# A two-layer encoder with four mixers: ten projection steps beside the scan, windowed attention and latent keys beside the latent attention

## The chip, the cores and the metric

The kernel runs on one core of a Trainium2 chip. The metric is the device time of one execution in microseconds (us). TensorE appears as PE (matmuls) and PEld (weight loads), VectorE as DVE, ScalarE as ACT, GpSimd as POOL, SyncE, which issues the DMAs here, as SP.

## The reference

1024 tokens of 1024 features pass through two layers in fp32. A layer projects its input once and hands the parts to four mixers of 256 features each; what follows (group norm, output projection, MLP, per-layer embedding) is not touched here.

```python
for i in range(DEPTH):                                  # 2
    u = h @ w_in[i]
    (cq, ckv, kr, hy_u, sq, sk, sv, ssd_z, ssd_xbc, ssd_dt) = jnp.split(u, IN_OFFSETS, axis=-1)
    y_a = mla_mixer(cq, ckv, kr, ...)                   # latent attention, 4 heads, all keys
    y_b = hyena_mixer(hy_u, ...)                        # two long convolutions by transforms
    y_c = swa_mixer(sq, sk, sv, ...)                    # windowed attention, 2 groups of keys, 4 heads
    y_d = ssd_mixer(ssd_xbc, ssd_dt, ...) * silu(ssd_z) # chunked scan, both directions
    y = group_rms_norm(concatenate([y_a, y_b, y_c, y_d]), mix_norm_g[i], 4)
    h = layer_norm(ALPHA * h + y @ w_out[i], ...)
    ...
```

Here mla normalises the latents (cq, ckv), projects them to queries, keys and values and attends over all 1024 keys; swa attends over 128 tokens to either side, with a sink; the scan works in 8 chunks of 128 tokens.

## The kernel before, in words

The kernel is written with generators: each mixer is a flow that yields between steps, `interleave` (L43) emits several flows in step with one another by the numbers of steps given with them, and `stagger` (L55) runs items of one flow one stage apart. A tile scheduler then reorders the instructions of each engine by its own model, within what the data and the buffers allow, so the emission is a wish and not the order.

`mixers` (L580) writes a layer's mixers as three stages. The **input stage** interleaves `hyena` with `proj`: 21 tiles of 128 features, each of 48 matmuls of 512 columns (`in_proj` L564; high and low parts of weights and activations make three products for each of 8 blocks and 2 halves) into a tile `pp` of 1024 columns; a row of 48 such products is named pp<-x,wh or pp<-x,wl. A tile is copied by ScalarE to `cv` and stored to DRAM (`plain` L607: L612; `latent` L615: L620, with token sums of squares `csq` on PE). T_Z (2 tiles) are the gates of the scan, T_CQ (2) and T_CKV (1) the latents of mla, T_SQ, T_SK, T_SV the input of swa, T_X, T_B, T_C that of the scan. Hyena ends with the product of `x2` and its result and two stores of y (L707).

The **scan stage** interleaves `ssd` (L822), `swa` (L1084) and `mla_keys` (L947), the latter held back by 34 empty steps. `ssd` loads xs, bs and cs again (L826) into tiles `xbc`; its first part, the states, makes token-major x and B (`xt`), `xd` = x by a decay, and their product; its second part, 16 outputs, makes Lm (exponentials), `wt` = the sum of two of them (one row wt<-Lm each), the products ps<-wt,xt, and an addition into xbc. Its tiles xbc, prev and xt come from the tag X of the pool `xp`, where the layer's input x also lies, and `PT` and `kT` of mla later. swa has two kv groups; each loads its rows, makes KH, KL and Q and then 8 blocks: scores in a `pp` tile (pp<-KH,Q), softmax (`ws`), transposes into another `pp` tile, `wpt`, and products with `sV`. `mla_keys` makes `kT` and `V` from the latent `ck`.

The **mla stage** interleaves `mla` (L984) with `out_ahead`, which prepares the output projection of Hyena's group. mla has 32 units (4 pairs of query tiles, 4 heads, 2 tiles): scores of 6 matmuls of 512 columns into a `pp` tile, maximum, `P` = exponentials (1024 columns), transposes (L1054), split into `PT`, and the products with V (L942).

PSUM: `one()` gives a `ps` tile of 512 columns out of 4 buffers, `two()` a `pp` tile of 1024 columns out of 2; projections, swa's scores and transposes and mla's scores all take `pp`. Weight rows are loaded to `wraw` (2 buffers) and split by POOL into `wh` and `wl` (`whl`, 4 buffers).

Of the kernel before, what the change touches and what calls it, by code (L numbers as in the profile page):

```python
# [10 lines left out]
F32 = mybir.dt.float32  # L11
# [6 lines left out]
RIGHT = "right"  # L18
# [10 lines left out]
# columns of the packed per-layer parameters  # L29
# [4 lines left out]
# feature tiles of the input projection  # L34
# [8 lines left out]
def interleave(*flows):  # L43
    """Emits flows, each (generator, number of its steps), in step with one another."""
    live = [[g, 0, n] for g, n in flows]
    while live:
        f = min(live, key=lambda f: f[1] / f[2])
        try:
            next(f[0])
            f[1] += 1  # L50
        except StopIteration:
            live.remove(f)


def stagger(items):  # L55
    """Emits the stages of items so that each item is one stage behind the one before it."""
# [18 lines left out]
class Trunk:  # L75
# [70 lines left out]
    def to_x_after(self, x, H, t0, t1, ins, pair=False):  # L146
        """Transposes token tiles t0 to t1, once the products up to ins have freed the tiles that the
        result goes to."""
# [11 lines left out]
    def layer_norm(self, h, gb, eps=None, first=None):  # L160
        """The statistics; returns two functions that normalise h in place, one after the other."""
# [16 lines left out]
        def affine(c=512):  # L178
            """The first c columns, scaled already, on GpSimd, the others on VectorE."""
# [74 lines left out]
    def embed(self):  # L254
        """Normalises the input; the second half of the tokens only when the function that is returned runs."""
# [43 lines left out]
    def sin_of(self, fp, out, pre):  # L299
        """out = sin(pre) with the argument brought to [-pi, pi]."""  # L300
# [99 lines left out]
    def bruun(self, pool, zm, zp, C):  # L400
        """Residues of a polynomial of 1024 coefficients (8 blocks of 128 rows, C columns each)
        modulo the eight factors of x^2048 - 1 of degree 256; zm and zp are its residues modulo
        x^1024 - 1 and x^1024 + 1."""
# [36 lines left out]
    def conv_fft(self, l, n, pool, z, feature_major, out):  # L440
        """Circular convolution of z (token-major, 8 x 256) with filter n, and the skip term that the
        filter holds; the result is token-major [128, 8 * 256] or feature-major [128, 2, 8 * 128]."""
# [112 lines left out]
    def in_half(self, x, w, ps, hf):  # L555
        c0 = hf * 512
        if not isinstance(w, tuple):
            # the products of the high and the low parts of the weights, in separate rows
# [5 lines left out]
    def in_proj(self, l, x, tile_i):  # L564
        """One tile of 128 features, [128, 1024] in PSUM, in two steps."""
# [7 lines left out]
    def conv3(self, out, ps, cw):  # L573
        """Centred 3-tap convolution along the free dim with bias: cw columns w0, w1, w2, b."""
# [4 lines left out]
    def mixers(self, l, x, mu, late, st0):  # L579
# [6 lines left out]
        res, sw = {}, ExitStack()  # L586
        ss = self.sm.tile([128, 4, 8], F32, name="ss")

        def scalars(su, ps):
            """Rotary key and dt, token-major."""  # L590
# [24 lines left out]
        def latent(pr, ti, k, rs, last, n):  # L615
            """A latent of attention with its gain, to DRAM; the sums of its squares go to rs."""
# [16 lines left out]
        def proj(pr, su, head, v, x1):  # L633
# [42 lines left out]
            for i in range(2):  # L676
                yield from plain(pr, T_SQ + i, qd[:, i])
                yield
            for i in range(2):
# [4 lines left out]
            yield from latent(pr, T_CKV, 2, res["rk"], True, 128)  # L684
            yield
            for i in range(2):
                yield from plain(pr, T_Z + i, zd[:, i], AF.Silu)
                yield
# [23 lines left out]
        with ExitStack() as ssu:  # L712
            with ExitStack() as st:
# [14 lines left out]
                interleave((hyena(st, v, x1), 54), (proj(pr, su, head, v, x1), 42))  # L728
            m1 = self.pool(st0, f"m1_{l}")
            w2 = self.pool(sw, f"w2_{l}", 2, side=RIGHT)  # L730
            att = {}
            with ExitStack() as st:
                mc = self.pool(st, f"mc{l}", 2)
                interleave((self.ssd(l, st, res["scal"], xbc, zd, yd[3]), 44), (self.swa(l, w2, yd[2], qd, kd, vd), 32),
# [1069 lines left out]
```

## Time and profile before

| what | value |
|---|---|
| median of 3 runs | 3237.84 us (3234.51 to 3241.9) |
| span of the profiled execution | 3236.6 us |
| difference of the median to that span | 1.2 us |
| PE busy, share of the span | 2976.9 us, 92% |
| VectorE, ScalarE, POOL | 76%, 40%, 56% |

The profile is of one execution; its span is the time that the sum is made against. A window is a stretch of the span in us from its start; the busy time of an engine in it says how much of it the engine worked, PEclk the share of full clock that was granted. A mark is one row of the timeline with its start.

### The profile page before, as it was taken

The numbers are of one execution on the slowest core, as the hardware profiler recorded it, in microseconds if no ns is written. First come the engines' busy times: TensorE is split into PE (matmuls) and PEld (weight loads), VectorE is DVE, ScalarE is ACT, GpSimd is POOL, SyncE is SP. The second block draws the span as 40 slices with busy tenths as digits, with TensorE's granted clock in tenths as the row PEclk, the third lists the DMA queues.
The fourth block names the chain that finished last, engine by engine and source line by source line (L and its number), as shares of the span: only waits on it lengthen the run. The fifth ranks groups of instructions, "written<-read, shape, count | busy, mean of one in ns | idle before, by whom it ended". The sixth has DMA issues, their size and how long they took to land.

```text
span 3236.6 us, 40462 instructions
## 1 busy us (share of the span) xinstructions
PE 2976.9 (92%) x14316; PEld 2429.1 (75%) x14316; DVE 2451.0 (76%) x3711; ACT 1292.0 (40%) x2278; POOL 1821.3 (56%) x1371
## 2 busy tenths in 40 slices
PE   6999989998999999999989998899989999989996
PEld 4887866877777777777868877778777777767685
DVE  7678776878765557999777786778786555689986
ACT  4332365743333334333343323667333333343341
POOL 5455533527656556886435454345177555578855
PEclk9999998999999999999999998999999999999998
DMA  5566523022222225313335755130222222343232
GB/s 178 156 200 204 192 75 130 16 83 85 85 79 78 78 79 198 123 47 115 126 100 172 225 192 165 53 121 25 97 85 79 79 78 78 114 163 107 74 135 92
DMA packets 140468, 368.98 MB, mean 114 GB/s; under 512 B 15139, under 2 KB 42023, under 8 KB 140009
## 3 DMA queue, kind: packets, MB, share of 16 engines
q1 hardware_dynamic: 126008, 315.72, 28.8%
q0 software_dynamic: 14256, 50.67, 5.2%
q8 instruction: 114, 1.87, 0.2%
q14 instruction: 90, 0.73, 0.1%
HBM read 278.77 MB, written 87.56 MB: 113 GB/s over the span
## 4 chain that ended last, share of the span: by engine, by line
PE 39%; DVE 21%; POOL 16%; issue 10%; DMA 10%; ACT 4%; SPq 0%; POOLq 0%; DVEq 0%; ACTq 0%
PE ps L99 18%; PE pp L99 13%; POOL w L87 5%; DMA wraw<-in_ffn_w_gate_dram 4%; POOL wraw L87 4%; DVE part L87 3%; POOL u L87 2%; DVE fr L87 2%; POOL H L87 2%; PE ps L942 2%; DVE H L90 2%; DVE s L87 1%; POOL part L87 1%; DVE H L87 1%; DMA wraw<-in_ffn_w_up_dram 1%
## 5 line engine op out<-in xcount | busy, mean ns | idle before, releaser
L99 PE MATMUL ps<-x,w 128*128 128x512 f32 x2112 | 508.2, 394 | 11.3 <-ACT v L84 6.1
L99 PEld LDWEIGHTS ps<-x,w 128*128 128x128 f32 x2112 | 400.1, 190 | 99.1 <-ACT v L84 7.0
L99 PE MATMUL pp<-x,wh 128*128 128x512 f32 x1344 | 427.9, 397 | 1.8 <-ACT wh L84 1.8
L99 PE MATMUL ps<-xq,w 128*128 128x512 f32 x1584 | 391.1, 397 | 29.7 <-DVE u L87 24.3
L1582 PE MATMUL ps<-part 128*128 128x512 f32 x1440 | 351.2, 399 | 33.8 <-DVE H L87 10.8
L99 PEld LDWEIGHTS ps<-xq,w 128*128 128x128 f32 x1584 | 292.9, 188 | 117.2 <-DVE u L87 50.7
L1582 PEld LDWEIGHTS ps<-part 128*128 128x128 f32 x1440 | 270.9, 191 | 110.5 <-DVE H L87 20.3
L99 PEld LDWEIGHTS pp<-x,wh 128*128 128x128 f32 x1344 | 254.9, 192 | 54.3 <-ACT wh L84 2.0
L87 POOL TENSOR_TENSOR w<-wraw,w 128x512 fp32r<-128x512 f32 x164 | 217.5, 1345 | 116.0 <-ACT w L84 116.0
L99 PE MATMUL pp<-x,wl 128*128 128x512 f32 x672 | 266.5, 397 | 3.8 <-POOL wl L87 3.8
L84 ACT ACTIVATE w<-wraw 128x512 fp32r<-128x512 f32 x264 | 151.8, 622 | 268.0 <-DMA wraw<-in_ffn_w_up_dram 218.6
L87 POOL TENSOR_TENSOR wl<-wraw,wh 128x1024 fp32r<-128x1024 f32 (+2 forms) x61 | 152.8, 2507 | 182.7 <-ACT wh L84 124.2
L87 POOL TENSOR_TENSOR part<-fr,part 128x512 fp32r<-128x512 f32 x120 | 192.4, 1628 | 47.2 <-ACT part L84 42.2
L87 DVE TENSOR_TENSOR s<-wraw 128x512 f32<-128x512 f32 x44 | 55.4, 1259 | 202.2 <-DMA wraw<-in_ffn_w_gate_dram 199.8
L99 PE MATMUL ps<-wo,yn 128*128 128x512 f32 x768 | 189.7, 405 | 5.4 <-DVE H L90 3.0
L1039 POOL TENSOR_TENSOR P<-P,smr 128x1024 f32<-128x1024 f32 x64 | 121.1, 1893 | 112.2 <-DVE smr L1038 103.3
L99 PEld LDWEIGHTS ps<-wo,yn 128*128 128x128 f32 x768 | 147.1, 195 | 39.4 <-DVE H L90 4.8
L90 DVE SCALAR_TENSOR_TENSOR g<-g,pp 128x1023 f32<-128x1023 f32 x88 | 126.6, 1439 | 57.7 <-ACT g L84 57.7
L87 POOL TENSOR_TENSOR u<-u,g 128x512 f32<-128x512 f32 x44 | 78.7, 1788 | 152.5 <-ACT g L84 152.3
L87 DVE TENSOR_TENSOR part<-wr,part 128x512 fp32r<-128x512 f32 x124 | 158.2, 1299 | 4.8 <-ACT part L84 4.8
L99 PE MATMUL ps<-wh,x 128*128 128x512 f32 x512 | 158.8, 391 | 0.0
L99 PEld LDWEIGHTS pp<-x,wl 128*128 128x128 f32 x672 | 128.5, 191 | 30.5 <-POOL wl L87 4.7
(381 smaller groups left out, 7038.7 us busy)
## 6 DMA issues: line engine op xcount, KB each, us to landing
c_fwd<-in_c_fwd_dram POOLq DMA_DIRECT2D x64, 512.0 KB, 5.1
wraw<-in_ffn_w_up_dram SPq DMA_DIRECT2D x50, 512.0 KB, 3.5
wraw<-in_ffn_w_gate_dram SPq DMA_DIRECT2D x44, 512.0 KB, 4.5
f<-u SPq DMA_DIRECT2D x88, 256.0 KB, 2.0
wraw<-in_w_in_dram SPq DMA_DIRECT2D x42, 512.0 KB, 4.1
fr<-f SPq DMA_DIRECT2D x40, 512.0 KB, 4.5
wr<-in_ffn_w_down_dram SPq DMA_DIRECT2D x36, 512.0 KB, 6.4
c_inv<-in_c_inv_dram POOLq DMA_DIRECT2D x32, 512.0 KB, 5.0
```

The costliest lines, as they stand in the source:

```text
L84: self.nc.scalar.activation(out, in_, func, **kw)
L87: (eng or self.nc.vector).tensor_tensor(out, a, b, op=op)
L90: return self.nc.vector.scalar_tensor_tensor(out, a, s, b, op0=op0, op1=op1)
L99: ins = self.nc.tensor.matmul(out, a, b, start=i == 0, stop=i == n - 1)
L942: ins = self.nc.tensor.matmul(out[0:64] if j else out, v[:, 0, :] if j else v.rearrange("p i d -> p (i d)"), terms[i][1 + j], start=k == 0 ...
L1039: nc.gpsimd.tensor_tensor(P, P, sm.to_broadcast([128, T]), op=ALU.mult)
L1582: nc.tensor.matmul(ps, u, v, start=k == 0 and (p != 1 or ch == 0), stop=k == 5 and (p != 1 or ch == last))
```

## The change

The five tiles T_Z, T_CKV and T_CQ (10 steps) leave `proj` for a flow `proj_late` that is emitted beside `ssd`. `ssd` gets a pool of its own (`sb`, seven tiles of 8 KB a partition) in place of the tag X, since the layer's input is still read beside it. swa and the latent keys leave the scan stage: the keys become the first part of the flow `attention`, and swa is a third flow beside it; the 34 empty steps go. The pools of swa, keys and mla are opened when those of the scan are closed. Comments are removed as well, which shifts the lines (L826 is L832, L707 is L710, L846 and L847 are L852 and L853, L942 is L948, L1016 is L1020, L1054 is L1058, L1094 is L1098, L1149 is L1153).

```diff
         def proj(pr, su, head, v, x1):
...
-            for i in range(2):
-                yield from latent(pr, T_CQ + i, i, res["rq"], i, 256)
-                yield
-            rq = res["rq"]
-            nc.vector.tensor_scalar(rq, rq, 96.0 ** -0.5, None, op0=ALU.mult)
-            yield from latent(pr, T_CKV, 2, res["rk"], True, 128)
-            yield
-            for i in range(2):
-                yield from plain(pr, T_Z + i, zd[:, i], AF.Silu)
-                yield
+
+        def proj_late(pr):
+            for i in range(2):
+                yield from plain(pr, T_Z + i, zd[:, i], AF.Silu)
+                yield
+            yield from latent(pr, T_CKV, 2, res["rk"], True, 128)
+            yield
+            for i in range(2):
+                yield from latent(pr, T_CQ + i, i, res["rq"], i, 256)
+                yield
+            rq = res["rq"]
+            nc.vector.tensor_scalar(rq, rq, 96.0 ** -0.5, None, op0=ALU.mult)
...
-                interleave((hyena(st, v, x1), 54), (proj(pr, su, head, v, x1), 42))
-            m1 = self.pool(st0, f"m1_{l}")
-            w2 = self.pool(sw, f"w2_{l}", 2, side=RIGHT)
+                interleave((hyena(st, v, x1), 54), (proj(pr, su, head, v, x1), 32))
+            with ExitStack() as st:
+                interleave((self.ssd(l, st, res["scal"], xbc, zd, yd[3]), 44), (proj_late(self.pool(st, f"pl{l}", 2)), 10))
+        rows, ahead = {}, {}
+
+        def attention(mc, m1, m2):
             att = {}
-            with ExitStack() as st:
-                mc = self.pool(st, f"mc{l}", 2)
-                interleave((self.ssd(l, st, res["scal"], xbc, zd, yd[3]), 44), (self.swa(l, w2, yd[2], qd, kd, vd), 32),
-                           (self.mla_keys(l, mc, m1, att, cd, res), 50))
-            sw.close()
-        rows, ahead = {}, {}
+            yield from self.mla_keys(l, mc, m1, att, cd, res)
+            yield from self.mla(l, m2, att, yd[0])
...
         with ExitStack() as sa:
+            w2 = self.pool(sa, f"w2_{l}", 2, side=RIGHT)
+            m1 = self.pool(sa, f"m1_{l}")
+            mc = self.pool(sa, f"mc{l}", 2)
             m2 = self.pool(sa, f"m2_{l}", 2)
-            interleave((self.mla(l, m2, att, yd[0]), 40), (out_ahead(), 36))
+            interleave((attention(mc, m1, m2), 48), (self.swa(l, w2, yd[2], qd, kd, vd), 44), (out_ahead(), 36))
...
     def ssd(self, l, ss, scal, xbc, zd, yd):
...
+        sb = self.pool(ss, f"sb{l}")
         for j in range(3):
-            pair = self.xp.tile([128, 2, T], F32, name="xbc", tag="X")
+            pair = sb.tile([128, 2, T], F32, name=f"xbc{j}")
...
-            prev.append(self.xp.tile([128, 8, 2, 128], F32, name="prev", tag="X"))
-            xt.append(self.xp.tile([128, 8, 2, 128], F32, name="xt", tag="X"))
+            prev.append(sb.tile([128, 8, 2, 128], F32, name=f"prev{g}"))
+            xt.append(sb.tile([128, 8, 2, 128], F32, name=f"xt{g}"))
...
     def mla_keys(self, l, mc, m1, att, cd, res):
...
-        for _ in range(34):
-            yield
```

How the instructions then stand on an engine is the scheduler's doing, and both layers read alike; the rows below are of layer 0. SP's queue at the end of the input stage, before (y is Hyena's result, sk, sq and sv the input of swa, xs, bs and cs that of the scan, kt a row of Hyena's filter spectra, ab a table of swa):

```order
L457 DMA kt<-khat_7_90 128x2x256
L620 DMA cq_275<-cv 128x1024
L1105 DMA wraw<-sk_273 64x1024 x2
L707 DMA y_267<-x_2609 256x1x512 x2
L1098 DMA ab<-in_c_alibi_dram 128x768
L1108 DMA wraw<-sq_272 128x1024
L612 DMA z_271<-cv 128x1024
L826 DMA xbc<-xs_276 128x1024 x2
L826 DMA xbc<-bs_277 128x1024 x2
L826 DMA xbc<-cs_278 128x1024 x2
```

and now:

```order
L457 DMA kt<-khat_7_90 128x2x256
L710 DMA y_267<-x_2402 256x1x512 x2
L832 DMA xbc_3203<-xs_276 128x1024 x2
L832 DMA xbc_3206<-bs_277 128x1024 x2
L832 DMA xbc_3209<-cs_278 128x1024 x2
L612 DMA z_271<-cv 128x1024 x2
L620 DMA cq_275<-cv 128x1024
L931 DMA wraw<-xs_276 128x1024
L620 DMA cq_275<-cv 128x1024
L929 DMA xbc_3209<-z_271 128x1024
```

swa's rows are gone from here, and the six loads of the scan stand directly behind the stores of y, ahead of the stores of two Z tiles and of the latents. Since the tile of xs lies where Hyena's x2 was, its load waits for the y stores.

PE at the same place. Before, the last 111 of Hyena's 640 products in the layer had 30 and 18 projection matmuls (and the sums csq) between them, and 96 behind the last. Now nothing stands between them. The two Z tiles are projected before them, in the input stage; the 144 matmuls of the three latent tiles stand behind the last product, 96 of them in five pieces (22, 4, 23, 27, 20) with the first transposes and state products of the scan between the pieces, the other 48 further on in the scan. PE's rows around the scan's first transposes (L852, L853), now:

```order
L99 MATMUL pp<-x,wl 128x512
L99 MATMUL pp<-x,wh 128x512
L852 MATMUL ps<-ident,xbc_3203 128x128 x2
L99 MATMUL pp<-x,wh 128x512
L99 MATMUL pp<-x,wl 128x512
L99 MATMUL pp<-x,wh 128x512 x2
L853 MATMUL ps<-ident,xbc_3206 128x128 x2
```

They stand behind 22 of the 96 here.

PE at the end of the scan, before (ps<-wt,xt: product of an output of the scan; L906: its transpose; L976: transposes of the keys; sV: products of swa; cn: queries):

```order
L1149 MATMUL pp<-ident,ws 128x128 x4
L99 MATMUL ps<-wt,xt 128x256
L976 MATMUL ps<-ident,ks 96x128 x4
L99 MATMUL ps<-wh,ck 128x512
L99 MATMUL ps<-wl,ck 128x512
L99 MATMUL ps<-wh,ck 128x512
L99 MATMUL ps<-wpt,sV 64x256 x3
L976 MATMUL ps<-ident,ks 96x128 x4
L99 MATMUL ps<-wpt,sV 64x256 x3
L976 MATMUL ps<-ident,ks 96x128 x4
L99 MATMUL ps<-wpt,sV 64x256 x5
L99 MATMUL ps<-wh,cn_5068 128x384
```

and now (csq: the sums of the latents; L1098: transposes of swa's values; ck: keys):

```order
L912 MATMUL ps<-ident,yo 128x128 x2
L99 MATMUL ps<-wt,xt_3218 128x256 x2
L912 MATMUL ps<-ident,yo 128x128
L99 MATMUL ps<-ones,csq 128x1 x4
L99 MATMUL ps<-wt,xt_3218 128x256
L99 MATMUL ps<-ones,csq 128x1 x4
L1098 MATMUL ps<-ident,wraw 128x128 x8
L99 MATMUL ps<-wh,ck 128x512
L99 MATMUL ps<-wl,ck 128x512
L99 MATMUL ps<-wh,ck 128x512 x2
L99 MATMUL ps<-wl,ck 128x512
L99 MATMUL ps<-wh,ck 128x512
L99 MATMUL pp<-KH,Q_4320 128x256
L99 MATMUL pp<-KL,Q_4320 128x256
```

No row of swa or of the keys stands before the scan's last product; their tiles (V, sV, Q, KH and others) lie on tiles of the scan. Behind it come swa's whole first kv group, 106 of swa's 204 matmuls as the rows count them, and the keys, and only then mla's first scores. The second kv group stands between mla's units:

```order
L99 MATMUL pp<-kT,qT_4805 128x512 x2
L99 MATMUL pp<-kT,qT_4806 128x512
L99 MATMUL pp<-kT,qT_4805 128x512 x2
L99 MATMUL pp<-kT,qT_4806 128x512
L99 MATMUL pp<-KH,Q_4846 128x384
L99 MATMUL pp<-KL,Q_4846 128x384
L99 MATMUL pp<-KH,Q_4847 128x384
L99 MATMUL pp<-KL,Q_4847 128x384
L1058 MATMUL ps<-ident,P 128x128 x16
L99 MATMUL pp<-kT,qT_4821 128x512 x2
L99 MATMUL pp<-kT,qT_4822 128x512
L99 MATMUL pp<-kT,qT_4821 128x512 x2
L99 MATMUL pp<-kT,qT_4822 128x512
```

In these rows the scores of a block of swa and the transposes of two units (L1058) stand between the scores of one unit of mla and those of the next. Before, mla's matmuls had nothing beside them but the queries and the sums of `out_ahead`. The eight loads of the residual for the output projection, which stood at mla's start in SP's queue, now stand late in mla, since their tiles lie where swa's are.

## Rows read from the trace of the kernel before

**Rows 1.** The page's busy time of each engine, us, share of the span and instructions.
```profile
PE 2976.9 (92%) x14316; PEld 2429.1 (75%) x14316; DVE 2451.0 (76%) x3711; ACT 1292.0 (40%) x2278; POOL 1821.3 (56%) x1371
```

**Rows 2.** Windows, layer 0: stretch, length, busy PE, PEld, DVE, ACT, POOL, PEclk, DMA, GB/s.
```profile
390.00:409.00 19.00, 17.96 (x87) 14.44 (x85) 8.28 (x20) 6.85 (x9) 6.07 (x7) 1.00 0.92 319
409.00:526.00 117.00, 101.21 (x565) 79.66 (x566) 88.97 (x300) 73.48 (x233) 39.47 (x42) 0.93 0.17 54
526.00:548.00 22.00, 17.38 (x64) 10.26 (x63) 12.44 (x26) 9.80 (x20) 9.06 (x6) 0.77 0.73 255
548.00:662.00 114.00, 109.52 (x720) 97.58 (x720) 94.47 (x187) 82.80 (x153) 61.25 (x37) 0.97 0.12 41
662.00:674.00 12.00, 10.12 (x65) 8.70 (x66) 9.06 (x14) 6.22 (x12) 3.60 (x3) 1.00 0.28 93
```

**Rows 3.** Timeline, marks of layer 0: start us, us, engine, line, operation, out<-in, shapes.
```profile
390.44 1.24 SPq L707 DMA_DIRECT2D y<-x  x2
...
409.10 0.43 DVE L87 TENSOR_TENSOR xd<-ps,s_w 128x256 f32<-128x256 f32 x1
...
525.47 0.29 DVE L87 TENSOR_TENSOR xbc<-ps,yt 64x128 f32<-64x128 f32 x1
...
547.59 1.20 ACT L84 ACTIVATE P<-pp,mx,rq 128x1024 f32<-128x1024 f32 x1 [5.03 <-issue]
...
673.97 0.45 SPq L1065 DMA_DIRECT2D y<-yt  x1
```

**Rows 4.** Windows of layer 1, the scan, same columns as rows 2.
```profile
2006.00:2123.00 117.00, 101.34 (x565) 79.54 (x564) 88.51 (x301) 73.52 (x233) 39.48 (x42) 0.91 0.18 55
```

**Rows 5.** Chain of waits, end of the input stage, layer 0: start us, us, what.
```profile
351.23 6.83 PE pp L99 x30
...
389.37 13.96 PE pp L99 x61
```

**Rows 6.** DMA issues from 385 to 412 us: KB each, median us to landing.
```profile
y<-x SPq DMA_DIRECT2D x2, 512.0 KB, 4.0
...
xbc<-bs SPq DMA_DIRECT2D x2, 512.0 KB, 8.9
```

**Rows 7.** Timeline of VectorE, four of the scan's 16 Lm sums.
```profile
443.04 0.41 DVE L87 TENSOR_TENSOR wt<-Lm 128x256 f32<-128x256 f32 x1
...
494.30 0.43 DVE L87 TENSOR_TENSOR wt<-Lm 128x256 f32<-128x256 f32 x1
...
504.10 0.43 DVE L87 TENSOR_TENSOR wt<-Lm 128x256 f32<-128x256 f32 x1 [0.67 <-PE ps L99]
...
511.84 0.43 DVE L87 TENSOR_TENSOR wt<-Lm 128x256 f32<-128x256 f32 x1
```

**Rows 8.** Waits of PE in the scan, 409 to 526 us: total, times, longest.
```profile
PE ps L99 <- DVE xd L87: 8.8, 4, 3.8
```

**Rows 9.** Timeline, the first and last rows of swa's first kv group.
```profile
405.07 0.36 PE L99 MATMUL pp<-KH,Q 128*128 128x256 f32 x1
...
446.29 0.81 ACT L84 ACTIVATE wpt<-pp 128x768 f32<-128x768 f32 x1 [1.37 <-PE ps L99]
```

**Rows 10.** Timeline of PE, swa's score, transpose and value matmuls.
```profile
422.12 0.34 PE L99 MATMUL pp<-KL,Q 128*128 128x384 f32 x1
422.29 0.33 PE L99 MATMUL pp<-KH,Q 128*128 128x384 f32 x1
...
434.46 0.82 PE L1149 MATMUL pp<-ident,ws 128*128 128x128 f32 x6
...
436.28 1.51 PE L99 MATMUL ps<-wpt,sV 128*64 128x256 f32 x6
```

**Rows 11.** Waits of PE beside mla, 548 to 662 us.
```profile
PE pp L99 <- ACT P L84: 4.9, 4, 2.8
```

**Rows 12.** Timeline, score matmuls of two of mla's units and the exponentials of the first.
```profile
548.94 5.49 PE L99 MATMUL pp<-kT,qT 96*128 96x512 f32 x12 [2.81 <-ACT P L84]
...
555.60 1.20 ACT L84 ACTIVATE P<-pp,mx,rq 128x1024 f32<-128x1024 f32 x1
```

More of the change, by code (lines that the diff above doesn't have):

```diff
@@ L585, in mixers @@
         xbc = [dr(n, [128, 2, T]) for n in ("xs", "bs", "cs")]
-        res, sw = {}, ExitStack()
+        res = {}
         ss = self.sm.tile([128, 4, 8], F32, name="ss")
```

## The prediction

> **What bounds the kernel now.** I read the page's busy shares first. TensorE (PE) is busy for 92% of the span, no other engine for more than 76% [rows 1], so a stage is as long as its matmuls plus the idle time of PE in it. The table of windows by stage comes next, layer 0 with its marks from the timeline [rows 2, 3]: PE is busy 17.96 of 19 us at the end of the input stage, 101.21 of 117 us in the scan, 17.38 of 22 us between the scan and the latent attention (mla), and 109.52 of 114 us in mla. Layer 1 reads the same (scan: 101.34 of 117) [rows 4]; I work out one layer and double it. The idle time that a better mixture could use is thus some 16 us in the scan and some 10 elsewhere. The clock that the throttle granted, 0.93 in the scan, 0.77 after it, 0.97 beside mla [rows 2], is lowest where PE has most idle time; a number below full speed is a mean of the 2.4 and the 1.2 GHz level.
>
> The marks of layer 0 are: y of Hyena goes to its store at 390.44, the first xd of the scan at 409.10, the scan's last addition 525.47, mla's first P (exponentials of a score tile) 547.59, the last store of mla 673.97 [rows 3]. I forecast each distance between two marks anew.
>
> **Term 1, up to the first xd.** The chain of waits at the end of the input stage runs through projections: 30 matmuls of 6.83 us, and later 96 behind the last inverse product of Hyena, the last 61 of them from 389.37 on [rows 5]. By the order, the last 111 Hyena matmuls had 30 and 18 projection matmuls between them; now none. The 96 behind the last inverse product are there still: the scheduler pulls two of the five "moved" tiles back. So 3 tiles (144 matmuls) move at all, and only 48 of them, at 6.83/30 = 0.228 us, 10.9 us in all, leave Hyena's path. The chain shows the 30 on it and not the 18, so I take 6.8 us off: Hyena's y goes out at 383.6. (Bounds: 0, if VectorE, which holds the chain in between, takes all of it, and 10.9.) Behind y SP's queue now holds the six scan loads at once, where a weight row, a table, a latent and one Z store stood between them; and the loads must wait for the y store, since their tile lies over x2. The y store takes 4.0 us from issue, a pair of xbc loads 8.9 beside the other traffic [rows 6]. With a DMA share of 0.92 there already [rows 2] I take 4.0 + 6.5 (8.9 less the two transfers that no longer share the queue) + 1 for transpose and copy: first xd at 395 instead of 409. **-14 us.** With 8.9 whole and only half of the 6.8 gained it would be -8; with all 10.9 gained -17.
>
> **Term 2, the scan.** From 409.10 to 525.47 it took 116.4 us [rows 3], with the swa steps and the latent keys on the same engines. Its own pace is seen where little stands beside it: the Lm sums, one for each of 16 outputs, come 3 intervals apart between 494.30 and 504.10, 3.27 us each; the states before them take 443.04 - 409.10 = 33.9 us [rows 7]. PE waited 8.8 us for xd there [rows 8], a chain through ScalarE and VectorE that swa's softmax lengthens. Without swa I put the states at 31, 15 intervals of 3.27 make 49, the addition and copies after the last output 7 (511.84 to 525.47 is 13.6 with swa and keys in between), and of the 48 moved matmuls' 10.9 us 8 that find no idle PE: 95 us. **-21 us.** Bounds: 85 (states 28, no cost for projections) and 110 (13.6 of tail stay, the interval is 4). The weight splits of the late tiles lie on GpSimd, busy 39.47 of 117 us [rows 2]; that is their cover, with much to spare.
>
> **Term 3, from the scan's end to mla's first P.** It was 22.1 us [rows 3], filled with the end of swa and of the keys. Now neither has begun when the scan ends: their pool lies on tiles of the scan that are still read, and by the order PE has no row of either before the scan's last matmul. Then the whole first kv group of swa, 106 of its 204 rows, stands ahead of mla's first scores. Beside the scan that group took 446.29 + 0.81 - 405.07 = 42 us [rows 9], call it 41. The scan is gone, but all the keys now stand in the same stretch. I take 5 for the transposes and splits of keys and queries, 40 for group and keys together, 4 for the first scores and their maximum: 49 us. **+27 us.** Bounds 40 (PE fed well by two independent flows) and 60 (the clock stays low as in the 0.77 stretch [rows 2]).
>
> **Term 4, mla itself.** It took 126.4 us to the last store [rows 3]. It now shares PE with the second kv group: 32 score matmuls 0.17 us apart, 44 transposes at 0.82/6 = 0.14, 44 value records at 1.51/6 = 0.25 [rows 10], so 5.4 + 6.0 + 11.1 = 22.5 us. Of PE's idle time there (114 - 109.5 = 4.5; the waits for P are 4.9 [rows 2, 11]) they can use 4.5 at most: 18. I add 5 for the score tiles, since swa takes its own from the same two PSUM buffers that mla's use. **+23 us.** Bounds 15 and 46. PE's busy time is the row against which I count room; the row beside it, of weight loads, has 97.58 of 114 us [rows 2]. The Trainium skill would have that one used: "Perfetto Trace Analysis" (Identifying the Most-Contended Engine) calls matmul busy time a poor measure of how near TensorE is to its limit, because matmuls are pipelined, and takes the busy share of weight loads. By it 16 us of mla would be free, term 4 would be 22.5 - 16 + 5 = +12, and the sum 3268 - 22 = 3246 us. No row here shows mla taking more work into those 16 us, so the sum goes by the matmul row. VectorE (94.47 of 114) and ScalarE (82.80) take swa's other half without becoming the bound. The weight and residual loads of the next stage, which stood at mla's start, wait for swa's pool now; beside mla the DMA share is 0.12 to 0.28 [rows 2], so I cost them at nothing; were that cover gone, one load pair's 8.9 us [rows 6] is the price.
>
> **The sum.** -14 - 21 + 27 + 23 = +15 per layer, +30 for two. The profiled span is 3236.6 us, 1.2 below the median of the three runs, 3237.84; 3236.6 + 30 + 1.2 = **3268 us**.
>
> **Rival 1: the two PSUM buffers bind.** mla makes a unit every 114/32 = 3.56 us [rows 2], and a score tile lives from the first of its matmuls (548.94) to the end of its P (555.60 + 1.20), 8 us [rows 12]: two buffers at 3.56 us each give 7.1, so they are full all the time. Then swa's second group does not slip in between; it holds the buffers as long as the first did, 41 us. Term 4 is +41, a layer +33, the time 3238 + 66 = 3304 us. Against it: PE's waits for P are 4.9 us only [rows 11], so the tiles live long because PE is busy. What the Trainium skill says in "Perfetto Trace Analysis" (Optimization Strategy) is on its side: the same gap repeated for a stretch can mean too little SBUF or PSUM for the next tile. The four waits of up to 2.8 us are such gaps, but few. Chance 0.17.
>
> **Rival 2, faster: two full mixtures.** PE was 96% busy beside mla (109.52/114) against 87% in the scan. From 390 to 674 PE's busy time is 17.96 + 101.21 + 17.38 + 109.52 + 10.12 = 256.2 us [rows 2]; with the 10.9 of the moved matmuls 267.1. If every stage were filled as mla was, they need 267.1/0.961 = 278 us, and from 383.6 the layer's mla ends at 661.6 instead of 674: -12.4 per layer, 3238 - 25 = 3213 us. It decides for this if term 3 is near 40 and term 4 below 20 while the scan takes 88. For it: projections have no chain of their own and fit any gap of the scan. Against: 106 rows of swa stand ahead of mla with a softmax chain and nothing but the keys beside it. The Trainium skill speaks for this rival ("Perfetto Trace Analysis", Optimization Strategy): where the most-contended engine changes over time, interleaving the regimes may help; here PE is first in every stage, so the rule bears on its idle time only. Chance 0.22.
>
> **Rival 3: it washes out.** Part of the change isn't carried out (two tiles of five stay where they were). With terms 3 and 4 nearer their lower ends, +18 and +15, a layer is -14 - 21 + 18 + 15 = -2, the time 3234 us. Chance 0.11.
>
> **Numbers.** The forecast has 0.50, the rivals 0.17, 0.22 and 0.11. What a measurement of this kernel can tell from no change is about 0.2%, 6.5 us. Faster by more: rival 2, and a little of rival 3: 0.23. Within: most of rival 3 and the near end of the forecast: 0.13. Slower: 0.64. The range goes from 3210 (just under rival 2) to 3306 (just over rival 1); what is left out is the forecast's tail with every term at its upper bound. The slower case alone would span 3248 to 3306.
>
> **What would show it.** In the changed profile: y of Hyena to its store some 7 us earlier than 390.44 (the input stage's own gain); first xd near 395; the scan about 95 us with short waits for xd; then a stretch of 45 to 50 us in which PE is busy for well under nine tenths and does swa and keys only; mla 150 us long with PE's waits for P grown above 4.9 us. I am wrong if the gap between the scan and the first P is nearer 30 (swa then did overlap), if the scan stays over 110 (then it had been bound by its own chain, not by its neighbours), or if PE beside mla stays as long as 126 us with swa in it.

## The result, and the profile after

The changed kernel takes 3327.78 us in the median of 4 runs (3323.24 to 3334.45), the kernel before 3236.18 us beside it: a ratio of 1.0284, 95% interval 1.0263 to 1.0306. It is slower, as forecast, but by some 92 us where I had 30, and outside the range (3210 to 3306). The page of the profiled execution, span and busy time, against [rows 1]:

```profile
span 3332.6 us, 40443 instructions
...
PE 3003.7 (90%) x14316; PEld 2441.2 (73%) x14316; DVE 2448.9 (73%) x3711; ACT 1292.1 (39%) x2278; POOL 1812.8 (54%) x1371
```

The instruction count of PE is the same, 14316. Its busy time grew by 3003.7 - 2976.9 = 27 us, though nothing was added, and the rest of the span, 3332.6 - 3003.7 = 329 us, is 69 us more than before (3236.6 - 2976.9 = 260). So 69 of the 96 us between the two profiled spans are time in which PE stands still; the other 27 are the same matmuls taking longer, in part at a lower granted clock (last section).

The marks of layer 0 on the timeline, which answer to [rows 3]:

```profile
397.26 1.22 SPq L710 DMA_DIRECT2D y<-x  x2
...
410.85 0.42 DVE L87 TENSOR_TENSOR xd<-ps,s_w 128x256 f32<-128x256 f32 x1 [13.61 <-ACT xt L84]
...
505.42 0.28 DVE L87 TENSOR_TENSOR xbc<-ps,yt 64x128 f32<-64x128 f32 x1 [0.38 <-PE ps L99]
...
568.50 1.20 ACT L84 ACTIVATE P<-pp,mx,rq 128x1024 f32<-128x1024 f32 x1 [4.45 <-DVE mx L1038]
...
726.70 0.45 SPq L1069 DMA_DIRECT2D y<-yt  x1
```

And the windows between them, columns as in [rows 2]:

```profile
397.00:411.00 14.00, 3.45 (x10) 2.47 (x11) 0.39 (x2) 0.57 (x2) 0.00 (x0) 0.63 0.77 254
411.00:506.00 95.00, 87.22 (x479) 73.33 (x477) 47.78 (x160) 39.09 (x122) 15.48 (x20) 0.95 0.22 75
506.00:568.00 62.00, 44.47 (x222) 31.28 (x221) 46.27 (x117) 40.60 (x100) 31.26 (x25) 0.89 0.38 107
568.00:727.00 159.00, 146.56 (x906) 123.65 (x907) 123.97 (x274) 105.47 (x210) 75.53 (x47) 0.96 0.16 53
```

Between Hyena's store and the first xd PE is busy 3.45 of 14 us, where it had 17.96 of 19; the scan is shorter; the hand-over to mla takes 62 us with PE busy 44.47 of them; mla takes 159 us at 146.56. Against the four terms of the prediction, with the same marks in layer 1 (before: last store of layer 0 at 673.97, then 2006.28, 2122.96, 2143.60, 2269.22; after: 726.70, then 2048.66, 2145.12, 2205.34, 2362.14):

| term, us per layer | forecast | layer 0 | layer 1 |
|---|---|---|---|
| 1, up to the first xd | -14 | +1.8 | -10.4 |
| 2, the scan | -21 | -21.8 | -20.2 |
| 3, scan's end to mla's first P | +27 | +41.0 | +39.6 |
| 4, mla | +23 | +31.8 | +31.2 |
| sum | +15 | +52.7 | +40.2 |

Layer 1's first term counts from the end of layer 0's mla, so it holds the rest of layer 0 as well. The two sums and 3 us behind the last mark are the 96 us. Over both layers the terms missed by 19 (term 1), 0 (term 2), 27 (term 3) and 17 us (term 4).

**Why the first term failed** is seen on PE. Its timeline behind Hyena's last product:

```profile
396.07 0.39 PE L99 MATMUL pp<-x,wh 128*128 128x512 f32 x1
406.03 0.66 PE L852 MATMUL ps<-ident,xbc 128*128 128x128 f32 x2 [9.57 <-DMA xbc<-xs]
406.34 0.78 PE L99 MATMUL pp<-x,wh 128*128 128x512 f32 x1
...
409.91 0.69 PE L853 MATMUL ps<-ident,xbc 128*128 128x128 f32 x2 [1.52 <-DMA xbc<-bs]
```

22 projection matmuls run, then stands the scan's transpose of xbc, which waits 9.57 us for its load, and behind it in PE's queue 122 projection matmuls that need none of these loads (emitted ahead of the transposes, they keep PE busy: "Late projections ahead of the scan" below). This is the order that the section on the change shows, and I read it as "the 96 are there still". The waits of PE from 340 to 411 us (total, times, longest) add others:

```profile
PE ps L852 <- DMA xbc<-xs: 9.6, 1, 9.6
PE ps L99 <- DMA c_inv<-in_c_inv_dram: 5.2, 1, 5.2
PE ps L99 <- ACT ph L84: 3.3, 1, 3.3
...
PE ps L99 <- ACT w L84: 1.4, 1, 1.4
```

The last three are Hyena's own: two steps on ScalarE (ph, w), and a load of its inverse transform, c_inv, 5.2 us, which the kernel before did not wait for here. GpSimd, and not SyncE, issues these loads; its timeline just before:

```profile
357.88 2.40 POOL L87 TENSOR_TENSOR wl<-wraw,wh 128x1024 fp32r<-128x1024 f32 x1 [5.29 <-ACT wh L84]
360.23 0.57 POOL L397 DMA_DIRECT2D c_fwd<-in_c_fwd_dram  x1
360.83 1.30 POOL L87 TENSOR_TENSOR rl<-v,rh 128x512 fp32r<-128x512 f32 x1
362.07 1.10 POOL L397 DMA_DIRECT2D c_inv<-in_c_inv_dram  x2
```

The weight split of a late tile (wl) stood 5.29 us for ScalarE's half, and the c_inv loads came behind it, at 362.07; PE, done at 362.5, went on at 367.75. With fewer projections between its products Hyena ran ahead of its loads here; whether this wait moved its end is taken up with the weight splits below.

### The profile page after: what moved, and what is told of

The parts are those of the page before. It is cut to its first block, busy times and chain, and to the rows that moved or that the text cites. A ratio compares the mean times of both kernels' runs of the same rounds, so it can differ in the third digit from the quotient of the medians.

```text
span 3332.6 us, 40443 instructions
## 1 busy us (share of the span) xinstructions
PE 3003.7 (90%) x14316; PEld 2441.2 (73%) x14316; DVE 2448.9 (73%) x3711; ACT 1292.1 (39%) x2278; POOL 1812.8 (54%) x1371
## 5 line engine op out<-in xcount | busy, mean ns | idle before, releaser
L99 PE MATMUL pp<-x,wh 128*128 128x512 f32 x1344 | 442.5, 406 | 12.2 <-ACT cv L84 6.3
L99 PEld LDWEIGHTS pp<-x,wh 128*128 128x128 f32 x1344 | 262.0, 197 | 68.3 <-ACT cv L84 6.9
```

Source lines behind the costliest of these rows:

```text
L99: ins = self.nc.tensor.matmul(out, a, b, start=i == 0, stop=i == n - 1)
```

## The experiments

All times are medians, with the kernel before measured on the same chip beside them (3230.97 to 3234.14 us). Windows are of layer 0, columns as in [rows 2].

**Attention and keys alone.** The kernel before, with windowed attention and the latent keys moved beside mla as in the change, and the projections left where they were. The 34 empty steps go here too.

```diff
-                interleave((self.ssd(...), 44), (self.swa(...), 32), (self.mla_keys(...), 50))
+                interleave((self.ssd(...), 44))
...
-            interleave((self.mla(l, m2, att, yd[0]), 40), (out_ahead(), 36))
+            interleave((attention(mc, m1, m2), 48), (self.swa(l, w2, yd[2], qd, kd, vd), 44), (out_ahead(), 36))
```

> Only windowed attention and the latent keys are moved; the projections stay in the input stage as before, with 96 of their matmuls between Hyena's last product and the scan. Theory A (moving the projections gained nothing, since Hyena's end is set by its own loads and VectorE steps; the whole loss is the hand-over, +41 us, and mla, +32 us per layer, less what the scan saves): input stage and first xd as before at 409, the scan near 87 us (95 less the 8 of late projections), so per layer -29 + 41 + 32 = +44, about 3324 us, within 10 us of the changed kernel. Rival B (the projections' move was worth the 14 us of my first term and the swa part cost more than thought): the changed kernel's gain is missing here, about 3350 us or more. Rival C (most of the loss is the projections'): near 3270 us.

Measured 3267.44 us against 3234.14, ratio 1.0103 (1.0086 to 1.0121).

```profile
395.00:408.00 13.00, 12.42 (x56) 9.89 (x55) 0.00 (x0) 2.11 (x3) 2.33 (x5) 1.00 0.91 322
408.00:471.00 63.00, 53.68 (x317) 43.40 (x316) 47.65 (x155) 32.68 (x113) 12.76 (x19) 0.98 0.19 64
471.00:531.00 60.00, 46.85 (x216) 33.60 (x216) 42.40 (x112) 41.00 (x100) 27.63 (x23) 0.85 0.40 116
531.00:690.00 159.00, 147.46 (x917) 125.72 (x918) 126.52 (x278) 106.72 (x211) 75.47 (x47) 0.97 0.17 55
```

Rival C holds: this half of the change costs 33 us, and moving the projections on top of it the other 60. (The projections' move with windowed attention still beside the scan was not run.) The scan without company takes 63 us, with PE busy 53.68 of them, not 87. The hand-over and mla are as long as in the changed kernel, so terms 3 and 4 belong to this half. Between Hyena's store and the scan PE is busy 12.42 of 13 us: the projections stand in front of the transposes here. From Hyena's last product to the first xd it takes 25.7 us, where it took 30.7 before and takes 25.5 in the changed kernel: what term 1 gained there came with this half, not with the projections.

**Projections back in the input stage, all else as changed.** Only the query latents are emitted late; the scheduler then puts all projections into the input stage. The scan keeps its own pool. (The line in brackets stands for the loops that move; the numbers of steps go with them.)

```diff
         def proj_late(pr):
-            (T_Z and T_CKV, back at the end of proj)
             for i in range(2):
                 yield from latent(pr, T_CQ + i, i, res["rq"], i, 256)
```

> The changed kernel with only the two query latents emitted late; the gates and the key latent are back in the input stage's flow. By the order all projection matmuls then stand in the input stage again, 72 of them behind Hyena's last product, none in the scan; the scan's own pool, the moved attention and the keys are as in the changed kernel. Theory A (the 144 matmuls cost their PE time, 33 us per layer, because the scan without windowed attention has no idle PE for them, while the input stage had): the scan falls from 95 to about 63 us, the time to about 3265 us, that of the kernel with only attention and keys moved. Rival (the scan's own pool, or loads that wait for Hyena's stores, cost the 60 us): it stays above 3310 us.

Measured 3265.64 us (ratio 1.0113, 1.0091 to 1.0135).

```profile
403.00:471.00 68.00, 61.31 (x353) 50.13 (x354) 48.73 (x161) 34.46 (x116) 13.96 (x19) 0.93 0.22 73
```

As theory A had it. The scan takes 68 us with PE busy 61.31; in the changed kernel 95 with 87.22. So 26 us of PE work came into the scan and 27 us of time. The pool and the loads behind Hyena's stores are cleared: they are in this kernel too.

**Late projections ahead of the scan.** The changed kernel, with eight of the ten late steps emitted before the scan, so that 144 matmuls stand in front of the transposes.

```diff
+                late_tiles = proj_late(...)
+                for _ in range(8):
+                    next(late_tiles)
-                interleave((self.ssd(...), 44), (proj_late(...), 10))
+                interleave((self.ssd(...), 44), (late_tiles, 2))
```

> The changed kernel with eight of the ten late projection steps emitted ahead of the scan, so that on PE almost all projection matmuls stand in front of the scan's first transposes, which wait for loads. Theory A (PE's idle 14 us there are a blocked queue: projections that could run stand behind transposes that wait): PE is busy in that stretch, the scan loses its projections and falls from 95 to some 85 us, 10 us less per layer, about 3312 us. Rival: the late projections fill idle time of the scan anyway, then the scan stays at 95 us and the time at 3330 us.

Measured 3325.5 us (3312.39 to 3329.06; ratio 1.0273, 1.0247 to 1.03), no clear difference to the changed kernel.

```profile
402.00:438.00 36.00, 32.06 (x153) 26.66 (x152) 1.28 (x6) 5.46 (x7) 4.07 (x2) 0.95 0.51 190
438.00:507.00 69.00, 60.30 (x339) 48.73 (x336) 47.99 (x159) 34.67 (x116) 13.92 (x19) 0.93 0.16 50
```

The mechanism is there: PE is busy 32.06 of 36 us ahead of the scan, and the scan takes 69. But the two stretches together, 105 us, are only 4 shorter than 14 + 95. Theory A's 10 us per layer were too many: the blocked queue idled PE for 10.6 us, but the projections that then ran ahead took longer (32 us) than the wait for the loads (14 us), so the scan began 22 us later after Hyena's store than in the changed kernel. The loss is less the queue than the work itself.

**Without windowed attention, in either kernel.** Two kernels that leave it out (its part of the output is zeros); the differences are its price in each place.

```diff
-(self.swa(l, w2, yd[2], qd, kd, vd), 44)
+(no_swa(), 1)      # one memset, two stores
```

> The changed kernel without windowed attention (its part of the output is zeros); the difference to the changed kernel is the price of windowed attention beside mla. Theory A (its chain and shared buffers cost more than its matmuls): the hand-over falls from 63 to some 35 us and mla from 158 to 126 us, 60 us per layer, about 3210 us. Rival (its price is its PE work alone, 22.5 us per kv group): 45 us per layer, about 3240 us.

> The kernel before without windowed attention (its part of the output is zeros); the difference to before is the price of windowed attention beside the scan. Theory A: the scan falls from 116 to some 87 us, 29 us per layer, about 3178 us, half of its price beside mla. Rival (it costs the same in either place and the loss lies elsewhere): 60 us per layer, about 3116 us.

Measured 3221.83 us for the changed kernel without it and 3171.44 us for the kernel before without it. So it costs 3327.78 - 3221.83 = 106 us beside mla and 3234.14 - 3171.44 = 63 us beside the scan, 53 and 31 us per layer. PE's busy time falls by 90 and 93 us, 22.5 and 23 us per kv group: its PE work was sized rightly, but beside the scan a third of it is hidden, and beside the keys and mla it costs more than its work. The hand-over and mla of the changed kernel without it:

```profile
502.00:544.00 42.00, 23.95 (x92) 16.14 (x91) 20.11 (x41) 17.82 (x45) 12.52 (x15) 0.73 0.61 214
544.00:669.00 125.00, 120.23 (x787) 106.76 (x787) 102.51 (x201) 88.28 (x162) 64.88 (x39) 0.97 0.08 22
```

The hand-over still takes 42 us, with PE busy 23.95: the keys and queries without windowed attention. The first kv group adds 20 us to that, for 20.5 us of PE work. But the eight residual loads of 512 KB are issued in this stretch again, from 503.59 us on (from 659.4 in the changed kernel), and the DMA share is 0.61 against 0.38; where they are not there, keys and queries take 32 us ("Windowed attention later" below), and by that the first group costs 30. Whether the loads make the 10 us was not separated. mla is 125 us, as before the change, so the second group is the whole +33 of mla. Of the kernel before without it:

```profile
411.00:487.00 76.00, 64.80 (x364) 51.62 (x365) 53.25 (x170) 39.28 (x134) 10.49 (x22) 0.92 0.14 52
487.00:516.00 29.00, 12.09 (x43) 8.60 (x43) 10.35 (x21) 10.35 (x23) 9.82 (x7) 0.65 0.70 254
```

With the keys beside the scan, scan and hand-over take 105 us. With the keys moved it would be 63 + 42 = 105 as well, an estimate from the scan alone of the first experiment and the hand-over above. By this estimate moving the keys costs nothing by itself. What this half of the change loses is the higher price of windowed attention, 53 - 31 = 22 us per layer; less the 5 us by which the first xd comes sooner behind Hyena, that makes 34 us for two layers, and 33 were measured.

**Own buffers for windowed attention.** The changed kernel, with the scores and transposes of windowed attention in `ps` tiles, so that mla has the two `pp` tiles alone.

```diff
-                ps, p2 = [], self.two()
+                ps = []
...
-                    ps.append(p2[:, h * 512:(h + 1) * 512])
+                    ps.append(self.one())
...
-                pt = self.two()
+                pt = [self.one() for _ in range((nk + 1) // 2)]
```

> The changed kernel with windowed attention's scores and transposes in tiles of the four 512-column buffers, so that mla has the two 1024-column buffers alone. Theory P (the two buffers bind when both share them): mla falls from 158 to some 145 us and the hand-over from 62 to 55, 20 us less per layer, about 3290 us. Theory A (beside mla windowed attention costs its PE work, and in the hand-over its chain): no more than 8 us either way, 3320 to 3335 us.

Measured 3339.38 us (ratio 1.0339, 1.032 to 1.0358), slower than the changed kernel, outside both expectations.

```profile
573.00:726.00 153.00, 142.53 (x901) 121.25 (x902) 123.81 (x269) 104.42 (x216) 75.56 (x47) 0.98 0.17 55
```

mla takes 153 us in place of 159, so leaving the two buffers to mla gained some 6 us per layer there, not the 13 of theory P, nor the 18 by which rival 1 stood above my term. That is a net figure, as mla's transposes and value products take the four `ps` buffers too: PE's waits of products into `pp` for P fell to 2.5 us beside mla, but 3.6 us of waits for yt, of transposes into `ps`, came in, and PE's idle time there fell only from 12.4 to 10.5 us. The hand-over grew from 62 to 68 us in layer 0 and from 60 to 71 in layer 1; the keys take `ps` tiles as well, but that this is the reason was not tested.

**Windowed attention later.** The changed kernel, with its flow held back by 20 steps.

```diff
-(self.swa(l, w2, yd[2], qd, kd, vd), 44)
+(swa_later(), 52)      # 20 empty steps, then self.swa
```

> The changed kernel with windowed attention held back by 20 steps, so that by the order both its key groups stand between mla's units and none before mla's first scores. Theory A (the hand-over is long because the first group's chain stands alone with the keys, PE idle for 17 of 62 us): the hand-over falls to some 33 us, mla grows by a group's PE work of 22 to 27 us to some 183 us, a few us less per layer, about 3315 us. Theory P (the shared buffers bind): mla grows by the 41 us that a group held them, to 199 us, 12 us more per layer, about 3350 us.

Measured 3344.48 us (ratio 1.0358, 1.0334 to 1.0382).

```profile
502.00:534.00 32.00, 21.61 (x101) 14.83 (x100) 18.59 (x38) 19.25 (x46) 14.93 (x16) 0.89 0.40 121
534.00:726.00 192.00, 173.08 (x1028) 140.95 (x1029) 151.72 (x353) 126.00 (x264) 88.60 (x56) 0.96 0.19 61
```

The hand-over fell to 32 us as expected, but mla grew to 192, 67 us more than without windowed attention: 33 us for each kv group, the second as much as the first. PE is busy 173.08 us there, 53 more than the 120.23 without it, and idle for the rest. The hand-over of 32 us holds the keys, the queries and only eight transposes of windowed attention. So a group costs 33 us beside mla and, against these 32 us, 30 beside the keys; the time lies between the two theories.

**Keys sooner.** The kernel before, with the keys held back by 20 steps in place of 34 (the flow's number of steps goes from 50 to 36).

```diff
-        for _ in range(34):
+        for _ in range(20):
```

> The kernel before with the latent keys held back by 20 steps in place of 34, so that they end within the scan. Theory A (the 22 us between the scan and mla's first exponentials, with PE at 17.6 us and a low clock, is a chain of keys and queries that could start sooner): the hand-over falls to some 15 us, 6 us less per layer, about 3222 us. Rival (the keys' PE work is only moved into a scan that has no room): the scan gets longer by as much, 3234 us.

Measured 3249.11 us (ratio 1.0057, 1.0034 to 1.0079): slower by 18 us.

```profile
417.00:538.00 121.00, 104.43 (x585) 79.41 (x586) 91.97 (x306) 77.09 (x243) 41.31 (x43) 0.94 0.19 57
538.00:557.00 19.00, 13.17 (x45) 9.00 (x43) 10.58 (x17) 4.83 (x9) 7.86 (x5) 0.73 0.65 213
```

The hand-over fell by only 3 us, and the scan grew by 4: the rival, and a little worse. By the marks the two stretches together grew by 2 us in layer 0 and 4 in layer 1; the rest of the 18 us was not traced.

**Weight splits of the late tiles on VectorE.** The changed kernel, with their low parts made there and not on GpSimd.

```diff
-        w, ps = self.in_start(l, tile_i)
+        w, ps = self.in_start(l, tile_i, eng)      # eng = nc.vector for the five late tiles
```

> The changed kernel with the low part of the five late tiles' weights made on VectorE in place of GpSimd. In the changed kernel PE waits 5.2 us for a c_inv load of Hyena's last part; GpSimd, which issues these loads, stood for 5.3 us at a weight split of a late tile just before. Theory Q (the blocked queue on GpSimd holds the loads up): the wait goes, Hyena's y leaves 4 to 6 us sooner, and as the rest is unchanged the time falls by 8 to 12 us, to some 3318 us. Rival (Hyena's end is set by its buffers and VectorE's steps, which now get more work): no gain or a loss, 3325 to 3340 us.

Measured 3320.14 us (ratio 1.0265, 1.0245 to 1.0286). The intervals overlap with the changed kernel's, so a gain of 6 to 8 us is possible and not shown. The wait for c_inv is gone from PE's list (330 to 395 us), and Hyena's y leaves at 391.74 us in layer 0, 5.5 sooner than in the changed kernel. But y leaves at 391.28 us in the changed kernel without windowed attention and at 391.90 in the one with it later, which have the wait still (5.1 and 5.7 us the longest). So the mechanism of theory Q, a load held up on GpSimd, is there, and that it sets Hyena's end is not shown. What PE waits for there now is Hyena's step ph on ScalarE and, behind Hyena's last product, cv, the copy of a projection:

```profile
PE ps L99 <- ACT ph L84: 4.6, 2, 4.3
PE pp L99 <- ACT cv L84: 3.2, 1, 3.2
```

**Gates first.** The kernel before, with only the order of its last five tiles turned round in the input stage: gates, key latent, query latents. The lines stand for the loops over the tiles.

```diff
+            (T_Z, T_Z)
+            (T_CKV)
             (T_CQ, T_CQ)
-            (T_CKV)
-            (T_Z, T_Z)
```

> The kernel before with only the order of the five tiles turned round in the input stage (the scan's gates, then the key latent, then the query latents), nothing moved out of it. In the kernel before PE waits 3.9 us per layer for the squares of a query latent that stand between Hyena's last products; by the order they now stand at the very end. Theory A (what helps the input stage is which projections fill Hyena's end, not that they leave): the wait goes and Hyena's y leaves some 4 us sooner per layer, 3226 to 3230 us. Rival (the squares now stand ahead of the scan's first products and block them there instead): no gain, 3234 us or more.

Measured 3227.15 us against 3232.95, in 12 and 17 runs, ratio 0.9979 (0.9968 to 0.9991): faster than the kernel before by 0.2%, and so than both. Of the kernel before this line of PE's waits (330 to 409 us) goes:

```profile
PE ps L99 <- ACT csq L84: 4.0, 1, 4.0
```

and ahead of the scan (385 to 412 us) come

```profile
PE pp L99 <- DVE Q L90: 5.9, 1, 5.9
PE ps L99 <- ACT csq L84: 1.7, 2, 0.9
```

So theory A holds in part. In layer 0 Hyena's last product comes 246.1 us after its first, not 250.7, and below the 250.2 to 252.5 of the four kernels with the input stage of before (that one, the one without windowed attention, attention and keys alone, keys sooner); in layer 1 it is 248.6 and not 252.2, but there those four spread from 247.6 to 252.2. Part of the gain goes to the wait of a first score product of windowed attention: from y to the first xd it now takes 21.0 us in layer 0, not 18.7.

## Why the prediction was wrong

**What bounds the kernel** was read rightly: PE is still busy for 90%, no other engine for more than 73%. What that reading did not tell is which idle time moved work can fill.

**Term 1 failed, and with it the direction of the projections' half.** "Only 48 of them leave Hyena's path" took 6.8 us off Hyena. It was no sooner: its y left at 397.26 us in layer 0 (390.44 before), and in layer 1 its last product came 253.6 us after its first (252.2 before), with 48 matmuls fewer up to there. The chain of waits had shown projections on the path only because they filled time in which Hyena waited for its next step; without them a load (5.2 us) and steps on ScalarE (3.3 and 1.4 us) ended the waits. A gain of 0 was in the text as a bound, though laid to VectorE. The other half of the term, the loads, came out nearly: 11.5 us forecast from y to the first xd, 13.6 measured, 18.7 before; but with only attention and keys moved it is 13.7 too. Behind Hyena's last product the "96 that are there still" did not cover the wait for the scan's loads any more, since 74 of them stood behind transposes that waited. The profile's 17.96 busy of 19 us [rows 2] was that cover; I named it, but did not cost its loss. That loss is small, though: with the queue unblocked the two stretches were only 4 us shorter. What the projections cost is their PE time in the scan.

**Term 2 came out by two errors that cancelled.** 95 us were forecast and measured. But I had 31 for the states, 49 + 7 for the outputs and their end, and 8 for the projections. Attention and keys alone give the scan by itself: its first xd at 408.36, first Lm sum at 421.82, sixteenth at 465.55, end at 471: 13.5 for the states, 43.7 for 15 intervals (2.92 each, 3.27 forecast) and 5.4. The other 32 us are projections at their full PE time. I had measured the states between rows where windowed attention stood in the same engines, and then taken almost nothing off; and "8 of 10.9 that find no idle PE" counted 48 matmuls where 122 went into or behind the scan's start. Moved work costs nothing only where PE would idle. The input stage had such time, the scan alone had 9 us of 63.

**Term 3: the keys.** 40 us for "group and keys together" was the step that failed; the term had 49 us, and 63 and 60 were measured. The keys and queries take 32 to 42 us by themselves, because none of it runs beside the scan's end any more; the group adds the other 20 to 30. The chain was the price, as the text argued against rival 2, but I had charged only one of the two flows for it. A wait of 8.1 us for Q near its start in layer 0 shows part of it (506 to 568 us):

```profile
PE pp L99 <- DVE Q L90: 8.1, 1, 8.1
```

**Term 4: size only.** The PE work was right (22.5 us a group, by the busy time of the kernels without it). It cost 33 us: mla's 4.5 idle us took nothing in, and some 10 us more were lost, of which own buffers gave some 6 back. My 23 credited the idle time and put 5 on the buffers. Of the 34 us between the windows of 159 and 125 us, 146.56 - 120.23 = 26 are PE busy and 8 idle. PE's waits beside mla, 568 to 727 us in the changed kernel, and 544 to 669 us without windowed attention (the last row), show the 8: with the waits for P from 1.7 to 4.9 us and two new ones, all of products into `pp` tiles.

```profile
PE pp L99 <- ACT P L84: 4.9, 4, 2.8
PE pp L99 <- ACT wpt L84: 2.2, 1, 2.2
PE pp L99 <- DVE wmx L1135: 2.2, 2, 1.2
...
PE pp L99 <- ACT P L84: 1.7, 3, 0.7
```

In the kernel before the waits for P were 4.9 us in layer 0 as well [rows 11], so they did not grow as the prediction's sign had it.

The weight-load row beside it would have given +12, further off. By the Trainium skill's rule ("Perfetto Trace Analysis", Identifying the Most-Contended Engine) there was, as the prediction estimated from it, room for 16 us; no run here found any.

**The rivals.** Rival 1 (buffers) falls as a mechanism of 18 us, since PE's idle time beside mla grew by 8; that its 3304 was nearest is luck. Rival 2 (two full mixtures) falls: PE was busy for 92% in the scan, yet for 72% in the hand-over. Rival 3 falls. The range failed because its upper end was rival 1, which moves term 4 alone: terms 1, 3 and 4 all came out longer at once. A case with the projections' cost at its full 33 us was in no rival.

What stays open is why a kv group costs 10 us more than its PE work beside mla. Waits of products into `pp` tiles are 8 us of it, but with own buffers others came in their place; and that PE is busy 26 us longer for 22.5 us of work was not explained. Hyena's end also differs by several us between profiles with the same order: y leaves at 390.44 us in the kernel before, 394.64 with attention and keys alone, 398.36 with the keys sooner, and at 391.28 to 397.26 in four kernels with the input stage of the changed one (that one, without windowed attention, own buffers, later). From its first product to its last Hyena takes 250.2 to 252.5 us in layer 0 in the old order and 252.1 to 257.5 in the changed one. So that it came no sooner is shown; how much later is known no better than that.

## What to carry to other kernels

Work that fills an engine's waits looks like work on its critical path; before moving it, read whether the engine would have been busy with something else, and price the move at the work's full time wherever the destination, measured without its old neighbours, has no idle time. Where an in-order queue now holds a waiting instruction in front of ready ones, count everything behind it (here it was worth 4 us of a layer). And when two things leave a stage at once, make the estimate for each of them alone: here a run with one half of the change gave its price and what the other half added, and the only gain, 0.2%, came from turning the order round inside the stage.

## What the runs showed of the hardware

Leaving PE idle made the remaining matmuls slower. In the changed kernel two projection products of the same form, 512 columns, take these times before and after the clock came back (PE's timeline, count at the end of the row):

```profile
391.62 1.05 PE L99 MATMUL pp<-x,wh 128*128 128x512 f32 x2
...
394.02 0.62 PE L99 MATMUL pp<-x,wh 128*128 128x512 f32 x2
```

1.05 us for two against 0.62; the products start 0.43 us apart in the one piece and 0.23 in the other. The granted clock of the two pieces is the last figure but two of these windows, about half and full, the levels of 1.2 and 2.4 GHz:

```profile
388.80:393.90 5.10, 5.01 (x12) 3.95 (x13) 5.10 (x5) 0.95 (x2) 3.27 (x3) 0.51 0.00 0
394.00:396.40 2.40, 2.40 (x11) 1.69 (x9) 2.40 (x1) 0.00 (x0) 2.40 (x4) 1.00 0.00 0
```

PE had idled 3.29 and 3.17 us shortly before the slow ones, and the granted clock is 0.63 in the window 397 to 411 above, 0.73 in the hand-over of the changed kernel without windowed attention, and 0.96 to 1.00 where PE is busy nearly all the time. Over the span its mean fell from 0.965 to 0.958. So part of what an idle stretch costs lies behind it; how much of the 27 us of longer busy time this makes was not separated from other causes.
